# A decoder trunk in split fp32: the order of the long and short products in the FFN's first projection

## The chip, the cores and the metric

The kernel runs on one core of a Trainium2 chip. The metric is device time in microseconds (us). The core has five engines with queues of their own: TensorE (PE in the profile; its weight loads are listed apart as PEld), VectorE (DVE), ScalarE (ACT), GpSimd (POOL) and SyncE (SP), which here only issues DMAs. Each engine takes its instructions strictly in the order that was fixed when the program was built.

## The reference

Two layers on a sequence of 256 tokens of width 1024, in float32. Layer 0 is half an FFN, a gated linear recurrence (HGRN2), half an FFN; layer 1 is half an FFN, dilated attention with shared keys and values, half an FFN. The change lies in the four FFNs:

```python
def _rms(x, gain):
    y = xf * lax.rsqrt(jnp.mean(xf * xf, axis=-1, keepdims=True) + EPS)
    return y * gain

def _swiglu(h, w_in, w_out):
    gate, up = jnp.split(h @ w_in, 2, axis=-1)
    return (jax.nn.silu(gate) * up) @ w_out

x = x + 0.5 * _swiglu(_rms(x, norm_gain[layer, 0]), ffn_w_in[layer, 0], ffn_w_out[layer, 0])
```

`w_in` is 1024 x 5632 (2816 gate columns, then 2816 up columns), `w_out` 2816 x 1024.

## The kernel before

**Split operands.** TensorE is fed with a rounded type (float32r), and the precision of float32 is kept by splitting every operand into a high half (rounded) and a low half (what rounding left). Of the four partial products three are made: high by high, low weight by high input, high weight by low input. A weight tile comes by DMA into a `raw` tile (line 242), ScalarE casts it to the high half `wh` (line 245), VectorE subtracts to get the low half `wl` (line 246). There are 4 `raw` buffers and 6 each of `wh` and `wl`; each holds 2 slices of 128 input channels by 512 columns. A buffer is taken again when its last reader is done: `raw` by the subtraction, `wh` and `wl` by the products. The input `xs` stands as `xs.hl`: per slice of 128 channels, 256 tokens of the high half beside 256 tokens of the low half.

**The first projection of an FFN** runs transposed (`linear_T`, line 275): weights are the stationary operand, tokens stream. It goes in 11 blocks (`c` in `ffn_within`, line 622), each of 256 gate and 256 up columns. A block's output is four accumulators of 128 columns, one PSUM bank each, in two pairs of a gate and an up bank (`spans`): pair 0 and pair 1. Each bank gets, for each of the 8 slices of channels, one *long* product (line 322; `wh` against `xs.hl`, 512 columns, which makes high by high in the bank's left half and high by low in its right half) and one *short* product (line 319; `wl` against the high half, 256 columns, added to the left half). That makes 32 longs and 32 shorts per block. The weights of a block come in four *parts* of two slices: parts 0 and 1 are called early, 2 and 3 late.

**Order of the products before.** In the first block of an FFN the order is special (`first_block` in the first FFN, the branch `norm.used == False` in the others, and in the second block of the first FFN). In every other block it is, for pair 0 and then for pair 1: 8 longs of the early parts, 16 shorts, 8 longs of the late parts. A pair's late longs and the early longs that follow them stand in a row, so PE runs 16 longs, 16 shorts, 16 longs, 16 shorts.

**After a pair's last product** `consume` (line 624) empties its banks: per bank a copy of the right half on ScalarE (line 458) and the addition of the left half on VectorE (line 459). These *sums* are `g` and `u`. Later come a multiplication on GpSimd (line 629), a SiLU on ScalarE (634), a product on GpSimd (635), and the split of the result into `hid` (216 and 217). These are put off by counted `tick()`s, which the product loops call; there are eight per block. The pool of accumulators has four banks, so a block's two pairs hold all of them, and the next block takes a bank when it has been emptied.

**What orders the engines' queues.** The instructions of an engine are put in order when the program is built, by a planner that takes what it thinks ready, what was written earlier first. `tc.issue_after(x)` keeps what is written inside it behind `x` on the engine of `x`. In `linear_T` the loads of part `n` stand inside such a block for every instruction in `norm.ahead[n]`, and `Norm.behind` (line 534) fills that list at the end of each block for the next one: the early parts come after the sums of the last pair of the block before the last (`made`), the late parts after the sums of pair 0 of the last block (`sums[0]`). Each list holds copies and additions, so it binds casts on ScalarE as well as subtractions on VectorE.

After the 11 blocks the second projection (`linear`, line 267, with `products`, line 252) uses the same buffers and banks. The recurrence's `linear_T` calls use the same function.

Of the kernel before, what the change touches and what calls it, by code (L numbers as in the profile page):

```python
# [19 lines left out]
P = 128  # L20
S = 256
NT = S // P
D = 1024
KD = D // P
# [3 lines left out]
NK = 2  # L28
# [75 lines left out]
def trunk(ctx, tc, x_in, norm_gain, ffn_w_in, ffn_w_out, a_w_in, a_lb_logits, a_out_gain, a_w_out,  # L104
          kv_norm, w_kv, k_gain, b_w_q, b_q_gain, b_w_o, rel_bias, c_onehot, c_masks, out):
    nc = tc.nc
# [87 lines left out]
    def tick():  # L194
        for job in pending:
            job[0] -= 1
        for job in [j for j in pending if j[0] <= 0]:
            pending.remove(job)
            job[1]()
# [49 lines left out]
    def accumulators():  # L249
        return [psa.tile([P, 512], F32, tag="acc", name=f"acc{t}") for t in range(NT)]  # L250
# [21 lines left out]
            part = load_part([(c0, v[:, k0 : k0 + nk, :]) for c0, v in columns], nk)  # L272
            products(xs, ps, k0, nk, nkt, *part, consume)

    def linear_T(norm, columns, spans, consume):


        xs = norm.sets[0][1]

        def load(k0):  # L280
            return load_part([(c0, v[:, k0 : k0 + NK, :]) for c0, v in columns], NK)

        starts = range(0, KD, NK)
        blocks, last = range(len(spans)), len(starts) - 1
        half = len(starts) // 2
        early, late = range(half), range(half, last + 1)


        parts = []
        for n, k0 in enumerate(starts):  # L290
            with ExitStack() as order:
                for ins in norm.ahead[n]:
                    order.enter_context(tc.issue_after(ins.ins))
                parts.append(load(k0))
        if norm.used:
            rows = []
            for i in blocks:
                rows += [("L", i, n) for n in early] + [("S", i, n) for n in range(last + 1)] + [("L", i, n) for n in late]
        else:

            rows = [(kind, i, n) for kind in "LS" for i in blocks for n in early]
            rows += [(kind, i, n) for i in blocks for kind in "SL" for n in late]
        norm.used = True
        sums = []


        banks = {}
        for kind, i, n in rows:
            if kind == "L" and n == 0:
                banks[i] = accumulators()  # L310
            ps = banks[i]
            wh, wl = parts[n]
            for k in range(NK):
                xs.need(n * NK + k)
            for c, acc in zip(spans[i], ps):
                for k in range(NK):
                    kk, w = n * NK + k, slice(c, c + P)
                    if kind == "S":
                        nc.tensor.matmul(acc[:, 0:S], wl[:, k, w], xs.h[:, kk, :], start=False, stop=False)  # L319
                    else:  # L320
                        hl = xs.hl[:, kk, :, :].rearrange("p a t -> p (a t)")
                        nc.tensor.matmul(acc, wh[:, k, w], hl, start=kk == 0, stop=kk == KD - 1)  # L322
            if kind == "L":
                if n == last:
                    sums.append(consume(i, ps))
                tick()
        norm.behind(sums)

    def first_block(norm, columns, spans, consume):

# [2 lines left out]
        gain, xs = norm.sets[0]  # L333
# [11 lines left out]
        banks = [accumulators(), [bank("first") for c in spans[1]]]  # L345
# [96 lines left out]
        sums = []  # L442
# [8 lines left out]
        half = KD // NK // 2  # L451
        norm.ahead = [ahead] * half + [ahead + [row] + sums[0] + sums[1]] * half
        norm.made = sums[1]

    def total(acc, pool, tag):

# [5 lines left out]
    class Norm:  # L462


        def __init__(self, x, sets, by_token=True, in_order=False, row_lag=ROW_LAG):
            self.x = x
            self.row_lag = row_lag
            self.spreads = by_token
            self.in_order = in_order
            self.used = False  # L470
            self.ahead = [[] for n in range(KD // NK)]
            self.made = []
            self.sets = [(g, Halves(act, KD, tag)) for g, tag in sets]
            self.fed = 0
            self.r = None
            self.by_token = None
            self.waiting = []
# [53 lines left out]
            if self.spreads and not self.in_order:  # L531
                defer(self.row_lag, self.spread)

        def behind(self, sums):


            half = KD // NK // 2
            self.ahead = [self.made] * half + [sums[0]] * half
            self.made = sums[-1]

        def halve(self):
# [76 lines left out]
    def ffn_within(x, pool, pool2, layer, f, norm, following):  # L618
        w_in = ffn_w_in[layer, f].rearrange("(k p) n -> p k n", p=P)
        hidden = Halves(pool, KF, "hid")  # L620

        for c in range(FC):

            def consume(i, ps, c=c):
                g, first = total(ps[0], pool2, "g")
                u, last = total(ps[1], pool2, "u")

                def scaled():
                    nc.gpsimd.tensor_tensor(g, g, norm.by_token, op=ALU.mult)  # L629
                    defer(SILU_LAG, gated)  # L630
                    defer(HIDDEN_LAG, put)

                def gated():
                    nc.scalar.activation(g, g, AF.Silu)  # L634
                    nc.gpsimd.tensor_tensor(u, u, g, op=ALU.mult)  # L635

                def put():
                    k = 2 * c + i
                    hidden.put(slice(k, k + 1), slice(0, S), u.unsqueeze(1))

                norm.with_rows(scaled)
                return first + last

            a, b = c * 256, DFF + c * 256
            spans = [(0, 256), (P, 256 + P)]
            if layer + f + c == 0:
                first_block(norm, w_in.rearrange("p k (s n) -> p k s n", s=2)[:, :, :, :256], spans, consume)
            else:
                linear_T(norm, [(0, w_in[:, :, a : a + 256]), (256, w_in[:, :, b : b + 256])], spans, consume)

        w_out = ffn_w_out[layer, f]

        def consume(n, t, ps):
            add_to_x(x, n, t, ps, following, norm.half[:, t : t + 1])
            if following is None:
                send(t, slice(n * 512, (n + 1) * 512), nc.sync)

        def send(t, cols, beside):
            for r, queue in enumerate((nc.sync, beside)):
                queue.dma_start(rows_of(out, 2 * t + r)[:, cols], x[64 * r : 64 * r + 64, t, cols])  # L660

        if following is not None:
            for n in range(2):
                linear(hidden, KF, [(0, half_of(w_out, n))], lambda t, ps, n=n: consume(n, t, ps))
            return
        linear(hidden, KF, [(0, half_of(w_out, 0))], lambda t, ps: consume(0, t, ps))


        ps = accumulators()
        parts = []  # L670
        tail = KF - 2 * NK
        for k in range(0, KF, NK):
            part = load_part([(0, half_of(w_out, 1)[:, k : k + NK, :])], NK)
            if k < tail:
                products(hidden, ps, k, NK, KF, *part, None)
            else:
                parts.append(part)
        for k in range(tail, KF):
            hidden.need(k)

        def rest(to, t, w, opens):
            tok = slice(t * P, (t + 1) * P)
            for kk in range(tail, KF):
                wh, wl = (v[:, (kk - tail) % NK, w] for v in parts[(kk - tail) // NK])
                nc.tensor.matmul(to, hidden.h[:, kk, tok], wh, start=opens and kk == tail, stop=False)
                nc.tensor.matmul(to, hidden.h[:, kk, tok], wl, start=False, stop=False)
                nc.tensor.matmul(to, hidden.l[:, kk, tok], wh, start=False, stop=kk == KF - 1)

        def add(t, c0, ps):
            xv = x[:, t, c0 : c0 + ps.shape[-1]]  # L690
            nc.vector.scalar_tensor_tensor(xv, ps, norm.half[:, t : t + 1], xv, op0=ALU.mult, op1=ALU.add)

        rest(ps[0], 0, slice(0, 512), False)
        add(0, 512, ps[0])
        send(0, slice(512, 1024), nc.sync)
        rest(ps[1][:, 0:256], 1, slice(0, 256), False)
        end = bank("end")[:, 0:256]
        rest(end, 1, slice(256, 512), True)
        add(1, 512, ps[1][:, 0:256])
        send(1, slice(512, 768), nc.sync)  # L700
        add(1, 768, ps[1][:, 256:512])
        add(1, 768, end)
        send(1, slice(768, 1024), nc.scalar)


    norm = Norm(x, [(gain_of(0, 0), "xT")], in_order=True)
# [34 lines left out]
    with ExitStack() as hgrn:  # L741
# [6 lines left out]
        w_in = a_w_in[0].rearrange("(k p) n -> p k n", p=P)  # L748
        xs = norm2.sets[0][1]
# [317 lines left out]
        norm = Norm(x_second, [(gain_of(0, 2), "xT")])  # L1067
# [9 lines left out]
    norm = Norm(x, [(gain_of(1, 1), "xT")], by_token=False)  # L1077
    ffn(x, 1, 0, norm2, norm)

    with ExitStack() as attn:  # L1080
# [73 lines left out]
        xs = norm.sets[0][1]  # L1154
# [295 lines left out]
```

## Time and profile before

| | us |
|---|---|
| median of 3 runs (least to most) | 1161.67 (1161.43 to 1161.83) |
| the profiled execution | 1161.63 |
| its span, first to last instruction | 1159.9 |
| TensorE busy | 1152.8 |
| VectorE busy | 781.2 |
| ScalarE busy | 706.8 |
| GpSimd busy | 227.7 |

The granted clock of TensorE was 1.0 on the whole. In the lines of the profile, `acc<-xT,wh x16` means 16 instructions in a row that write an accumulator from `xT` (or `xK`: the input) and `wh`; the first two numbers of a timeline row are the start and the time from the first start to the last end in us; a bracket gives idle time of the engine just before, and what ended it. Matmuls overlap at their ends, so a product's duration is longer than the spacing from one start to the next; the spacing is what counts. L322 is line 322 of the listing.

### The profile page before, as it was taken

Reading aid. Unit: us, or ns where it says so; the run is one execution under the profiler, and the core shown is the slowest. Engines: PE = TensorE matmul, PEld = TensorE weight load, DVE = VectorE, ACT = ScalarE, POOL = GpSimd, SP = SyncE. Lnnn points to the kernel's source line nnn. Section 1 sums busy time; section 2 is a strip of 40 time slices with the busy share of each in tenths; the row PEclk is TensorE's granted clock in tenths of the full one; section 3 lists DMA queues with packets and bytes.
Section 4 is the critical chain, followed back from the end, with each engine's and each line's share of the span. In section 5 each row is a group of like instructions: output and inputs, shape, how many; then the busy total and the mean of one; then the engine's idle time right before and its main releaser. Section 6 shows DMA issues by size and latency. Waiting matters only on the chain.

```text
span 1159.9 us, 18928 instructions
## 1 busy us (share of the span) xinstructions
PE 1152.8 (99%) x6781; PEld 973.1 (84%) x6781; DVE 781.2 (67%) x1276; ACT 706.8 (61%) x1263; POOL 227.7 (20%) x243
## 2 busy tenths in 40 slices
PE   9999999999999999999999999999999999999998
PEld 7888888888888888888888887888877778888887
DVE  6766655898577666657667556866866865766752
ACT  6665555876566655556656446557767775665631
POOL 2323201310023331003333002231210100332300
PEclk9999999999999999999999999999999999999999
DMA  8766656644457666556665666565555453766661
GB/s 254 223 183 200 209 186 191 183 160 164 127 167 212 186 198 203 185 158 202 183 196 190 210 184 190 172 195 176 156 165 152 138 153 103 222 183 183 198 221 54
DMA packets 181731, 209.23 MB, mean 180 GB/s; under 512 B 15499, under 2 KB 139987, under 8 KB 181636
## 3 DMA queue, kind: packets, MB, share of 16 engines
q1 hardware_dynamic: 181008, 207.61, 58.1%
q8 instruction: 53, 0.87, 0.3%
q10 hardware_dynamic: 628, 0.40, 0.1%
q14 instruction: 42, 0.34, 0.1%
HBM read 205.82 MB, written 1.10 MB: 178 GB/s over the span
## 4 chain that ended last, share of the span: by engine, by line
PE 94%; DVE 2%; DMA 1%; ACT 1%; issue 0%; POOL 0%; SPq 0%; DVEq 0%; ACTq 0%; POOLq 0%
PE acc L322 28%; PE acc L260 15%; PE acc L319 15%; PE acc L262 14%; PE acc L261 14%; DVE wl L246 1%; PE ob L1406 1%; DMA raw<-in_ffn_w_in_dram 1%; PE tpn L1148 1%; PE tpp L1381 1%; PE tp L493 1%; ACT wh L245 1%; PE ob L1002 0%; PE wps L162 0%; PE sp L1331 0%
## 5 line engine op out<-in xcount | busy, mean ns | idle before, releaser
L246 DVE TENSOR_TENSOR wl<-raw,wh 128x1024 fp32r<-128x1024 f32 x380 | 479.7, 1271 | 225.4 <-ACT wh L245 163.3
L245 ACT CAST wh<-raw 128x1024 fp32r<-128x1024 f32 x380 | 397.0, 1050 | 198.5 <-PE acc L262 161.1
L322 PE MATMUL acc<-xT,wh 128*128 128x512 f32 x1152 | 278.4, 392 | 0.0
L322 PEld LDWEIGHTS acc<-xT,wh 128*128 128x128 f32 x1152 | 211.0, 188 | 40.5
L319 PEld LDWEIGHTS acc<-xT,wl 128*128 128x128 f32 x1152 | 147.8, 191 | 6.7 <-DVE wl L246 1.0
L319 PE MATMUL acc<-xT,wl 128*128 128x256 f32 x1152 | 150.1, 283 | 0.6 <-DVE wl L246 0.5
L260 PE MATMUL acc<-wh,hid 128*128 128x512 f32 x344 | 134.2, 390 | 0.0
L262 PE MATMUL acc<-wh,hid 128*128 128x512 f32 x344 | 134.2, 390 | 0.0
L261 PE MATMUL acc<-wl,hid 128*128 128x512 f32 x344 | 133.8, 389 | 0.0
L629 POOL TENSOR_TENSOR g<-g,row 128x256 f32<-128x256 f32 x88 | 67.0, 762 | 274.8 <-DVE g L459 256.3
L635 POOL TENSOR_TENSOR u<-u,g 128x256 f32<-128x256 f32 x88 | 89.9, 1022 | 47.0 <-ACT g L634 47.0
L574 POOL TENSOR_TENSOR rs<-var,mhalf 128x8 f32<-128x8 f32 (+1 forms) x32 | 48.5, 1516 | 229.2 <-DVE var L572 229.2
L260 PE MATMUL acc<-wh,xK 128*128 128x512 f32 x224 | 92.2, 412 | 0.0
L262 PE MATMUL acc<-wh,xK 128*128 128x512 f32 x224 | 88.1, 393 | 0.0
L261 PE MATMUL acc<-wl,xK 128*128 128x512 f32 x224 | 87.7, 392 | 0.0
L458 ACT COPY g<-acc 128x256 f32<-128x256 f32 x103 | 37.9, 372 | 80.6 <-PE acc L322 79.4
L322 PE MATMUL acc<-xK,wh 128*128 128x512 f32 x352 | 84.9, 392 | 0.0
L260 PE MATMUL acc<-wh,xT 128*128 128x512 f32 x192 | 77.7, 405 | 0.0
L262 PEld LDWEIGHTS acc<-wh,hid 128*128 128x128 f32 x344 | 64.6, 188 | 13.4
L260 PEld LDWEIGHTS acc<-wh,hid 128*128 128x128 f32 x344 | 64.6, 188 | 13.3
L261 PEld LDWEIGHTS acc<-wl,hid 128*128 128x128 f32 x344 | 64.6, 188 | 13.2
L262 PE MATMUL acc<-wh,xT 128*128 128x512 f32 x192 | 75.3, 393 | 0.0
(207 smaller groups left out, 1403.6 us busy)
## 6 DMA issues: line engine op xcount, KB each, us to landing
raw<-in_ffn_w_in_dram SPq DMA_DIRECT2D x344, 256.0 KB, 3.9
raw<-in_ffn_w_out_dram SPq DMA_DIRECT2D x88, 512.0 KB, 4.5
raw<-in_w_kv_dram SPq DMA_DIRECT2D x72, 256.0 KB, 4.2
raw<-in_a_w_in_dram SPq DMA_DIRECT2D x32, 512.0 KB, 4.3
raw<-in_b_w_q_dram SPq DMA_DIRECT2D x24, 512.0 KB, 3.7
raw<-in_w_kv_dram SPq DMA_DIRECT2D x48, 128.0 KB, 2.4
raw<-in_a_w_out_dram SPq DMA_DIRECT2D x8, 512.0 KB, 4.7
raw<-in_b_w_o_dram SPq DMA_DIRECT2D x8, 512.0 KB, 3.6
```

Source lines behind the costliest of these rows:

```text
L245: nc.scalar.copy(wh[:, :nk, :], raw[:, :nk, :])
L246: nc.vector.tensor_tensor(wl[:, :nk, :], raw[:, :nk, :], wh[:, :nk, :].bitcast(F32), op=ALU.subtract)
L260: nc.tensor.matmul(ps[t], xs.h[:, kk, tok], wh[:, at, :], start=kk == 0, stop=False)
L261: nc.tensor.matmul(ps[t], xs.h[:, kk, tok], wl[:, at, :], start=False, stop=False)
L262: nc.tensor.matmul(ps[t], xs.l[:, kk, tok], wh[:, at, :], start=False, stop=kk == nkt - 1)
L319: nc.tensor.matmul(acc[:, 0:S], wl[:, k, w], xs.h[:, kk, :], start=False, stop=False)
L322: nc.tensor.matmul(acc, wh[:, k, w], hl, start=kk == 0, stop=kk == KD - 1)
L458: copied = nc.scalar.copy(y, acc[:, S : 2 * S])
L493: nc.tensor.transpose(tp[:, c * P : (c + 1) * P], self.x[:, t, at : at + P], ident)
L574: nc.gpsimd.tensor_tensor(r[:, :n], v[:, :n], mhalf[:, :n], op=ALU.pow)
L629: nc.gpsimd.tensor_tensor(g, g, norm.by_token, op=ALU.mult)
L635: nc.gpsimd.tensor_tensor(u, u, g, op=ALU.mult)
```

## The change

In the FFNs' first projection, from the third block of each FFN on (`norm.blocks > 1` at entry), the products are issued by a new function: all 32 longs first, bank by bank (8 slices into one bank, then the next bank, through both pairs), then all 32 shorts, bank by bank; each pair's `consume` comes after its own shorts. `norm.blocks` counts the blocks of an FFN. The recurrence's calls keep the old order.

`behind` changes what the late parts of the next block come after, for blocks that are followed by a block of the new kind: no longer all four sums of pair 0, but only the very last sum of the block (`sums[-1][-1:]`), an addition on VectorE. So the late subtractions follow the block's last sum, and the late casts on ScalarE have no such order any more. `tick()` is called after every four longs, eight times per block, and not among the shorts.

```diff
-    def linear_T(norm, columns, spans, consume):
+    def linear_T(norm, columns, spans, consume, in_rows=False):
...
+        if in_rows and norm.blocks > 1:
+            return whole_rows(norm, parts, spans, consume)
...
-        norm.behind(sums)
+        norm.behind(sums, in_rows)
+
+    def whole_rows(norm, parts, spans, consume):
+
+        xs = norm.sets[0][1]
+        banks = []
+        for pair in spans:
+            ps = accumulators()
+            banks.append(ps)
+            for c, acc in zip(pair, ps):
+                for kk in range(KD):
+                    hl = xs.hl[:, kk, :, :].rearrange("p a t -> p (a t)")
+                    nc.tensor.matmul(acc, parts[kk // NK][0][:, kk % NK, c : c + P], hl, start=kk == 0, stop=False)
+                    if kk % 4 == 3:
+                        tick()
+        sums = []
+        for i, (pair, ps) in enumerate(zip(spans, banks)):
+            for c, acc in zip(pair, ps):
+                for kk in range(KD):
+                    nc.tensor.matmul(
+                        acc[:, 0:S], parts[kk // NK][1][:, kk % NK, c : c + P], xs.h[:, kk, :], start=False, stop=kk == KD - 1
+                    )
+            sums.append(consume(i, ps))
+        norm.behind(sums, True)
...
-        def behind(self, sums):
+        def behind(self, sums, in_rows):
...
             half = KD // NK // 2
-            self.ahead = [self.made] * half + [sums[0]] * half
+            self.blocks += 1
+            late = sums[-1][-1:] if in_rows and self.blocks > 1 else sums[0]
+            self.ahead = [self.made] * half + [late] * half
             self.made = sums[-1]
...
-                linear_T(norm, [(0, w_in[:, :, a : a + 256]), (256, w_in[:, :, b : b + 256])], spans, consume)
+                linear_T(norm, [(0, w_in[:, :, a : a + 256]), (256, w_in[:, :, b : b + 256])], spans, consume, True)
```

`first_block` sets `norm.blocks = 1`, and `Norm` starts it at 0.

More of the change, by code (lines that the diff above doesn't have):

```diff
@@ L453, in first_block @@
         norm.made = sums[1]
+        norm.blocks = 1
     def total(acc, pool, tag):
@@ L472, in __init__ @@
             self.made = []
+            self.blocks = 0
             self.sets = [(g, Halves(act, KD, tag)) for g, tag in sets]
```

## The prediction

> **What bounds the kernel now.** I read the page first: busy times, granted clock, the chain that ended last.
>
> ```profile
> span 1159.9 us, 18928 instructions
> PE 1152.8 (99%) x6781; PEld 973.1 (84%) x6781; DVE 781.2 (67%) x1276; ACT 706.8 (61%) x1263; POOL 227.7 (20%) x243
> ...
> PEclk9999999999999999999999999999999999999999
> ...
> PE 94%; DVE 2%; DMA 1%; ACT 1%; issue 0%; POOL 0%; SPq 0%; DVEq 0%; ACTq 0%; POOLq 0%
> PE acc L322 28%; PE acc L260 15%; PE acc L319 15%; PE acc L262 14%; PE acc L261 14%; DVE wl L246 1%; PE ob L1406 1%; DMA raw<-in_ffn_w_in_dram 1%; PE tpn L1148 1%; PE tpp L1381 1%; PE tp L493 1%; ACT wh L245 1%; PE ob L1002 0%; PE wps L162 0%; PE sp L1331 0%
> ```
>
> TensorE makes up 94% of the chain at full clock, and the two lines that the change reorders, the long products (L322) and the short ones (L319), hold 43% of it. A reordering of PE's work can win only what PE loses between its products. So the second view is the timeline of PE in steady blocks of the first FFN, and narrow windows of it; a clipped window shows the first start, and the time to the last end, of the products inside it. The two rows with slashes are the products' durations (least/median/most, ns).
>
> ```profile
> 66.21 2.08 PE L319 MATMUL acc<-xT,wl 128*128 128x256 f32 x16
> 68.12 3.82 PE L322 MATMUL acc<-xT,wh 128*128 128x512 f32 x16
> 71.77 2.08 PE L319 MATMUL acc<-xT,wl 128*128 128x256 f32 x16
> 73.69 3.82 PE L322 MATMUL acc<-xT,wh 128*128 128x512 f32 x16
> ...
> 69.51 2.43 PE L322 MATMUL acc<-xT,wh 128*128 128x512 f32 x10
> 72.13 1.72 PE L319 MATMUL acc<-xT,wl 128*128 128x256 f32 x13
> 73.69 1.32 PE L322 MATMUL acc<-xT,wh 128*128 128x512 f32 x5
> L322 PE MATMUL acc<-xT,wh x1152: 387/389/499, 19.8 to 633.1; 128*128 128x512 f32 x192
> L319 PE MATMUL acc<-xT,wl x1152: 277/283/386, 23.5 to 631.4; 128*128 128x256 f32 x192
> ```
>
> From start to start, a settled long product takes (2.43 - 0.389) / 9 = 0.2268 us, a short one (1.72 - 0.283) / 12 = 0.1198 us. The first five longs after a run of shorts are slower: (1.32 - 0.389) / 4 = 0.2328 us. So a run of 16 longs takes 71.77 - 68.12 = 3.65 us where 16 settled ones would take 3.63, and a run of 16 shorts takes 1.91 to 1.92, which is 16 x 0.1198. Is the excess paid for each switch or for each product? Runs of other lengths tell, in the second block of the first FFN:
>
> ```profile
> 23.49 3.04 PE L319 MATMUL acc<-xT,wl 128*128 128x256 f32 x24
> 26.36 2.00 PE L322 MATMUL acc<-xT,wh 128*128 128x512 f32 x8
> 28.20 1.11 PE L319 MATMUL acc<-xT,wl 128*128 128x256 f32 x8
> ```
>
> Eight longs take 28.20 - 26.36 = 1.84 us against 8 x 0.2268 = 1.81: the same 0.02 to 0.03 us as for sixteen. Twenty-four shorts take 2.87 us, 24 x 0.1198. A switch from shorts to longs costs some 0.022 us, the other way nothing. That is all that PE loses in a steady block; there is no wait in it.
>
> ```profile
> 64.39:75.52 11.13, 11.13 (x65) 9.84 (x64) 7.40 (x11) 6.84 (x13) 3.55 (x4) 1.00 0.64 189
> ```
>
> In this row of the table by stages (stretch, us, then busy PE, PEld, DVE, ACT, POOL, clock, DMA share, GB/s) one block of 11.13 us has PE busy throughout, VectorE for 7.40 and ScalarE for 6.84 us. They have room, but their deadlines move.
>
> **The change, part by part.**
>
> *Order of the products.* Nothing is added or removed: 32 longs and 32 shorts per block, as before, with the same operands; ticks stay at eight per block, so the deferred steps come up in the same blocks. Before, PE switches to longs twice per block (once per pair), afterwards once. Blocks 2 to 10 of each of the four FFNs take the new path: 9 x 4 = 36. Gain: 36 x 0.022 = 0.8 us (0.7 to 0.9 by the two runs above). Eight products in a row now add to one bank, where it was two; the settled pace is the same across a change of bank as within one, so I cost that at nothing.
>
> *Emptying the banks.* Before, pair 0's banks are emptied under pair 1's 32 products. Now the shorts of all four banks come last, and the next block begins on bank 0 at once. The rows: one bank is emptied by ScalarE's copy and VectorE's addition.
>
> ```profile
> 64.20 0.37 ACT L458 COPY g<-acc 128x256 f32<-128x256 f32 x1 [1.20 <-PE acc L322]
> 64.60 0.42 DVE L459 TENSOR_TENSOR g<-acc,g 128x256 f32<-128x256 f32 x1
> ```
>
> From copy to free bank: 64.60 + 0.42 - 64.20 = 0.82 us. Set the start of a new-style block at 0. Its longs end at 32 x 0.2268 + 0.022 = 7.28, its shorts at 7.28 + 32 x 0.1198 = 11.11. Bank 0's last short ends at 7.28 + 7 x 0.12 + 0.283 = 8.40, and the bank is free at about 9.3 if ScalarE and VectorE are: 1.8 us before the next block wants it. Bank 3's last sum is done at about 11.28 + 0.1 + 0.82 = 12.2, 1.1 into the next block, which wants that bank only after 24 longs (5.4 us). The cover is 1.8 us at bank 0 and 4.3 at bank 3; what lies past it would stall PE in every one of 36 blocks.
>
> *The low halves.* In steady blocks the two late casts and subtractions run before the block that uses them:
>
> ```profile
> 71.83 1.03 ACT L245 CAST wh<-raw 128x1024 fp32r<-128x1024 f32 x1
> 72.89 1.22 DVE L246 TENSOR_TENSOR wl<-raw,wh 128x1024 fp32r<-128x1024 f32 x1 [1.90 <-PE acc L319]
> 73.09 1.05 ACT L245 CAST wh<-raw 128x1024 fp32r<-128x1024 f32 x1
> 74.37 1.22 DVE L246 TENSOR_TENSOR wl<-raw,wh 128x1024 fp32r<-128x1024 f32 x1
> ```
>
> The block that needs them starts at 75.52. Now these subtractions wait for the last sum and run from 1.1 to 3.6 us into their block; its shorts begin at 7.28, so 3.7 us of cover remain. The bracket in the row at 72.89 shows why they must be moved: they reuse buffers that the shorts release, and the shorts now end the block. Queued behind them on VectorE are the next block's two early subtractions and two `hid` ones; four subtractions from 1.1 on end at 1.1 + 4 x 1.22 = 6.0, which leaves 2.9 us for the small ones until bank 0's sum at 8.9. Behind them on SyncE are the reloads of their `raw` buffers, some 3.6 us later in the block than now. The late casts lose their order behind pair 0's copies and are bound only by their buffers, which the last bank's longs release at about 6.1 and 6.5; the first longs that use them come at 0.9 and 1.4 of the next block, where the old order gave until 3.7. In steady blocks 73.09 + 1.05 = 74.14 is early enough. I cost all this at nothing.
>
> *The third block of the second FFN* is not steady:
>
> ```profile
> 346.29 3.82 PE L322 MATMUL acc<-xT,wh 128*128 128x512 f32 x16
> 349.95 2.46 PE L319 MATMUL acc<-xT,wl 128*128 128x256 f32 x16
> ...
> 351.66 0.74 PE L319 MATMUL acc<-xT,wl 128*128 128x256 f32 x4
> ...
> 352.24 0.40 PE L322 MATMUL acc<-xT,wh 128*128 128x512 f32 x1
> 349.11 1.05 ACT L245 CAST wh<-raw 128x1024 fp32r<-128x1024 f32 x1
> 350.39 1.22 DVE L246 TENSOR_TENSOR wl<-raw,wh 128x1024 fp32r<-128x1024 f32 x1
> ```
>
> Its shorts wait for the last part's subtraction (done at 351.61, they go on at 351.66): 352.24 - 349.95 = 2.29 us instead of 1.92, a loss of 0.4 that vanishes, since the shorts now come 5.5 us later. But its longs, which start at 346.29 + 1.84 = 348.13, want that last part's cast after six products, at 349.5, and the cast ends at 350.16: a new wait of 0.7 us, unless it is moved forward. Between 0 and 0.7 I take 0.7, where the row puts it. At the other third blocks the same casts end in time, and the waits in second blocks stay.
>
> **Sum**, on the profiled execution's 1161.63 us (its span of 1159.9 and 1.7 around it; 0.04 below the median of the runs): 1161.63 - 0.8 - 0.4 + 0.7 = 1161.1 us. What a measurement of this kernel can tell from no change is about 0.2%, 2.3 us, so this is no change.
>
> **Rivals.** *The switch is worth nothing.* If the slow first longs belong not to the switch but to what runs beside them, or if the planner mixes shorts among the longs, the 0.8 falls away: 1161.63 - 0.4 + 0.7 = 1161.9 us. Against it: the excess is alike behind 8, 16 and 24 shorts. [...]
>
> *Bank 0 is not free: slower.* The place is ScalarE's queue late in a block. A late cast can stand there ahead of bank 0's copy and wait for its `raw` tile. The rows are the issue of a load on SyncE's queue (ns), and how long loads take from issue to landing, first in steady blocks, then over the whole kernel (least/median/most):
>
> ```profile
> L242 SPq DMA_DIRECT2D raw<-in_ffn_w_in_dram x344: 367/370/1497, 8.5 to 1074.3; - x172
> ...
> DMA to landing us min/median/max: 2.9/3.8/5.0
> DMA to landing us min/median/max: 2.2/3.9/6.0
> ```
>
> The second late subtraction ends at 3.6; its buffer's two loads are issued at about 3.7 and, 0.37 later, 4.1; with 3.8 us the tile lands at 7.9, the cast ends at 8.95, and bank 0 is free at 9.8, in time. With 5.0 it is 11.0, just in time. It decides from a landing of 5.1 us on; at 5.6 each block loses 0.46 us, 36 x 0.46 = 17 us: 1178. For it: four reloads now follow each other closely, at 1.2 us apart, while before they came in pairs. Against it: the medians, and that the copy may stand ahead of the cast. The Trainium skill ("Trainium Kernel Development and Optimization", Best Practices) warns that consistent bubbles can mean that SBUF or PSUM ran out; all four banks are taken by one block here, and no run so far shows a bubble from it.
>
> *Much faster* would need more than PE loses. The waits left in second blocks are these:
>
> ```profile
> 340.15 0.74 PE L319 MATMUL acc<-xT,wl 128*128 128x256 f32 x4 [0.50 <-DVE wl L246]
> 987.86 0.74 PE L319 MATMUL acc<-xK,wl 128*128 128x256 f32 x4 [0.83 <-DVE wl L246]
> ```
>
> The change does not touch these blocks (0.5 + 0.8 us), and what it does touch is 0.8 + 0.4 = 1.2 us. Only a shift in other stages, through another plan, could give more than 0.2%.
>
> **How the numbers follow.** Forecast 0.62; switch worth nothing 0.18; bank 0 late 0.16; a windfall elsewhere 0.04. The first two are within 0.2%, the third above, the fourth below, so faster 0.04, same 0.80, slower 0.16. The forecast's own range is 1160.1 (the cast moves forward, and the switch is worth 0.9, with 0.2 for other stages) to 1162. For 8 in 10 the range takes in the second case and the mild end of the third (0.1 us per block, 3.6 us): 1159.9 to 1165.
>
> **What would show it.** In the changed profile: runs of 32 L322 and 32 L319 in the timeline of PE, a block of 11.11 us, the first five longs of a run slow only once per block. The third block of the second FFN: full pace in its shorts, a wait for the last cast (L245) after six longs. VectorE's late L246 pair straight behind the last L459 of a block. Wrong would be an idle PE ahead of the first long of each block, released by `g` L459 (bank 0), or by `wh` L245, or shorts that wait for L246.

## The result and the profile after

The changed kernel takes 1243.15 us (median, 1241.42 to 1248.07); the kernel before takes 1161.55 (1160.92 to 1161.83) beside it. The ratio is 1.0709, 95% interval 1.0696 to 1.0722: 81.6 us slower, where 1161.1 and no change had been forecast. The profiled execution took 1244.82 us, which is 83.2 more than the profiled one of before.

The same lines of the page as for the kernel before (span, busy times, the chain by engine):

```profile
span 1243.1 us, 19031 instructions
PE 1175.7 (95%) x6781; PEld 983.3 (79%) x6781; DVE 785.1 (63%) x1276; ACT 702.9 (57%) x1263; POOL 238.4 (19%) x243
...
PE 51%; DMA 16%; DVE 11%; ACT 8%; POOL 7%; issue 6%; SPq 1%; ACTq 0%; POOLq 0%; DVEq 0%
```

PE, at 94% of the chain before, holds 51% now. What came in is DMA, VectorE, ScalarE and GpSimd together: a chain that passes through all of them. The view of waits names its joints (who waited for whom: us in total, times, longest):

```profile
PE acc L341 <- DVE g L485: 45.9, 25, 3.6
PE acc L260 <- DVE g L485: 8.9, 4, 2.7
PE acc L260 <- DVE u L485: 3.2, 4, 1.1
...
ACT wh L245 <- DMA raw<-in_ffn_w_in_dram: 120.0, 68, 3.5
```

The first long of a block (L341 in the changed listing) waits for the sum of bank 0 (L485, `g`): the sign that the prediction had named as the one that would prove it wrong. ScalarE's casts wait 120.0 us for tiles of `w_in`; before it was 9.0 us in 11 waits (`ACT wh L245 <- DMA raw<-in_ffn_w_in_dram` there too). The stretches between the first longs of two neighbouring blocks (columns as in the prediction's row) show that PE is idle for 1.82 us of 13.22 in the first, and that none of the other engines is busy for much more than half of it (PEld is PE's own weight loads):

```profile
70.05:83.27 13.22, 11.40 (x65) 9.90 (x65) 7.52 (x11) 6.72 (x12) 3.81 (x4) 1.00 0.56 169
83.27:96.66 13.39, 13.02 (x64) 11.03 (x65) 7.51 (x11) 6.70 (x12) 3.79 (x4) 0.87 0.52 155
```

From the first long of an FFN's third block (its first L341) to the first product of its second projection (L260), the four FFNs take 119.5, 122.4, 116.7 and 117.5 us: 476.1 for 36 blocks, 13.22 each. Before, the same four stretches took 401.2. That is 75.0 of the 83.2 us. It holds the 8.9 us in the second row of the waits, which end at those first products; the 3.2 of the third row come on top. Of the remaining 5.0 some 3 lie in the second projection of the last FFN, where the granted clock stood at 0.50 for 6.83 us (more on that at the end); the rest is spread over the stages around.

Where the loop runs is seen in the timeline of one block, from one copy of bank 0 to the next:

```profile
68.22 1.04 ACT L245 CAST wh<-raw 128x1024 fp32r<-128x1024 f32 x1 [1.74 <-DMA raw<-in_ffn_w_in_dram]
69.17 0.36 ACT L484 COPY g<-acc 128x256 f32<-128x256 f32 x1
...
70.05 7.57 PE L341 MATMUL acc<-xT,wh 128*128 128x512 f32 x32 [1.71 <-DVE g L485]
...
70.91 0.42 ACT L664 ACTIVATE g<-g 128x256 f32<-128x256 f32 x1 [1.10 <-POOL g L659]
71.23 0.36 ACT L484 COPY g<-acc 128x256 f32<-128x256 f32 x1
...
72.18 0.41 ACT L216 CAST hid<-u 128x256 fp32r<-128x256 f32 x1 [0.59 <-POOL u L665]
...
72.49 0.36 ACT L484 COPY u<-acc 128x256 f32<-128x256 f32 x1
...
73.14 0.41 DVE L485 TENSOR_TENSOR u<-acc,u 128x256 f32<-128x256 f32 x1
...
73.47 2.88 DVE L246 TENSOR_TENSOR wl<-raw,wh 128x1024 fp32r<-128x1024 f32 x2
...
76.42 0.37 SPq L242 DMA_DIRECT2D raw<-in_ffn_w_in_dram  x1
...
76.83 0.47 SPq L242 DMA_DIRECT2D raw<-in_ffn_w_in_dram  x1
...
81.44 1.04 ACT L245 CAST wh<-raw 128x1024 fp32r<-128x1024 f32 x1 [2.00 <-DMA raw<-in_ffn_w_in_dram]
82.39 0.36 ACT L484 COPY g<-acc 128x256 f32<-128x256 f32 x1
```

Read it as a round. The copy of bank 0 goes at 69.17. ScalarE takes the copies of pair 1 only behind pair 0's SiLU (L664) and split (L216), each of which waits for GpSimd, so bank 3's copy goes at 72.49: 3.32 us. The last sum (L485, `u`) comes behind it, and the two late subtractions run from 73.47 to 76.35: 3.86 us more. The second one frees a `raw` tile; its two loads are issued at 76.42 and 76.83: 0.48. The cast that waits for that tile goes at 81.44, 4.61 later, and the next copy of bank 0, which stands behind this cast on ScalarE, at 82.39, 0.95 later. 3.32 + 3.86 + 0.48 + 4.61 + 0.95 = 13.22 us: the block. TensorE needs 11.11 us for its products and waits for the rest. No single engine is slow; a chain of small steps returns to its own beginning, and going round it takes longer than the block. There are 28 such rounds, from the third to the tenth block of the four FFNs. Four of the five terms are the same in nearly all of them, to within 0.05 us. The fifth, from the second issue to the cast, goes from 4.07 to 6.42 us (4.61 in the mean), and it makes one round 12.7 us long and another 15.0.

### The profile page after: what moved, and what is told of

Read it like the earlier page. It is cut to its first block, busy times and chain, and to the rows that moved or that the text cites. A ratio compares the mean times of both kernels' runs of the same rounds, so it can differ in the third digit from the quotient of the medians.

```text
span 1243.1 us, 19031 instructions
## 1 busy us (share of the span) xinstructions
PE 1175.7 (95%) x6781; PEld 983.3 (79%) x6781; DVE 785.1 (63%) x1276; ACT 702.9 (57%) x1263; POOL 238.4 (19%) x243
## 4 chain that ended last, share of the span: by engine, by line
PE 51%; DMA 16%; DVE 11%; ACT 8%; POOL 7%; issue 6%; SPq 1%; ACTq 0%; POOLq 0%; DVEq 0%
PE acc L260 13%; PE acc L262 13%; PE acc L261 13%; DMA raw<-in_ffn_w_in_dram 12%; POOL u L665 5%; DVE wl L246 5%; PE acc L324 4%; ACT wh L245 3%; DMA raw<-in_ffn_w_out_dram 3%; PE acc L321 2%; POOL g L659 2%; DVE g L485 1%; DVE u L485 1%; SPq L242 1%; ACT g L484 1%
## 5 line engine op out<-in xcount | busy, mean ns | idle before, releaser
L245 ACT CAST wh<-raw 128x1024 fp32r<-128x1024 f32 x380 | 397.3, 1050 | 338.3 <-PE acc L262 132.8
L341 PE MATMUL acc<-xT,wh 128*128 128x512 f32 x864 | 212.5, 405 | 36.7 <-DVE g L485 35.3
L341 PEld LDWEIGHTS acc<-xT,wh 128*128 128x128 f32 x864 | 165.8, 194 | 77.2 <-DVE g L485 39.4
L485 DVE TENSOR_TENSOR g<-acc,g 128x256 f32<-128x256 f32 x103 | 43.1, 422 | 186.3 <-ACT g L484 186.3
L260 PE MATMUL acc<-wh,hid 128*128 128x512 f32 x344 | 136.3, 396 | 12.1 <-DVE g L485 8.9
L262 PE MATMUL acc<-wh,hid 128*128 128x512 f32 x344 | 135.2, 393 | 0.0
L665 POOL TENSOR_TENSOR u<-u,g 128x256 f32<-128x256 f32 x88 | 101.1, 1150 | 61.2 <-DVE u L485 28.0
L348 PEld LDWEIGHTS acc<-xT,wl 128*128 128x128 f32 x864 | 107.2, 192 | 2.1
L348 PE MATMUL acc<-xT,wl 128*128 128x256 f32 x864 | 107.8, 283 | 0.0
L260 PE MATMUL acc<-wh,xK 128*128 128x512 f32 x224 | 92.3, 412 | 0.0
L260 PEld LDWEIGHTS acc<-wh,hid 128*128 128x128 f32 x344 | 65.1, 189 | 28.2 <-DVE g L485 9.7
L341 PE MATMUL acc<-xK,wh 128*128 128x512 f32 x288 | 69.8, 400 | 11.0 <-DVE g L485 10.6
L260 PE MATMUL acc<-wh,xT 128*128 128x512 f32 x192 | 77.8, 405 | 0.0
```

What stands on the lines that cost most here:

```text
L245: nc.scalar.copy(wh[:, :nk, :], raw[:, :nk, :])
L260: nc.tensor.matmul(ps[t], xs.h[:, kk, tok], wh[:, at, :], start=kk == 0, stop=False)
L262: nc.tensor.matmul(ps[t], xs.l[:, kk, tok], wh[:, at, :], start=False, stop=kk == nkt - 1)
L341: nc.tensor.matmul(acc, parts[kk // NK][0][:, kk % NK, c : c + P], hl, start=kk == 0, stop=False)
L348: nc.tensor.matmul(acc[:, 0:S], parts[kk // NK][1][:, kk % NK, c : c + P], xs.h[:, kk, :], start=False, stop=kk == KD - 1)
L485: return y, [copied, nc.vector.tensor_tensor(y, acc[:, 0:S], y, op=ALU.add)]
```

## The experiments

Theory A is that loop. It has four links: the late casts stand ahead of the copies; the late subtractions follow the last sum; late and early parts share four `raw` tiles; SiLU and split stand between the copies. Cutting or shortening any link should bring the block back to 11.11 us, and lengthening one should lengthen the block by as much. Theory B: four banks are too few where 32 shorts end a block, whatever the other engines do. Theory C: the reloads of `raw` are too crowded, since all four come after the last sum. The first four kernels ran beside each other, and so did the last three; the kernel before took 1161.75 us beside the first and 1161.58 beside the others.

**Late low halves after the first sums.** The new order of the products, with the old rule for the late parts.

```diff
-            late = sums[-1][-1:] if in_rows and self.blocks > 1 else sums[0]
+            late = sums[0]
```

> The new order of products, but the late parts' casts and subtractions come after the four sums of pair 0 again, as before. Theory A (the loop: on ScalarE the late casts now stand ahead of bank 0's copy and wait for raw tiles that come free only after the block's last sum, so that the time around, 13.2 us, takes the place of the block's 11.1): the copies of banks 0 and 1 come first again, a block takes 11.1 us, 1160 to 1164 us in all. Theory B (four banks: closing all four at the end of a block leaves too little time to empty them, whatever ScalarE's order): no better than 1230. Theory C (the four reloads in a row crowd each other and land late): one subtraction moves ahead, so perhaps half is won, about 1200.

Measured: 1166.07 us, ratio 1.0035 (1.0022 to 1.0048). The second link and the first are cut: the late casts are back behind pair 0's copies. A steady block, and the copy and sum of its bank 0:

```profile
63.73:74.85 11.12, 11.12 (x67) 9.85 (x66) 8.42 (x11) 6.53 (x13) 4.85 (x4) 1.00 0.65 191
```

```profile
63.73 7.44 PE L341 MATMUL acc<-xT,wh 128*128 128x512 f32 x32
...
72.22 0.37 ACT L484 COPY g<-acc 128x256 f32<-128x256 f32 x1 [2.60 <-PE acc L348]
72.63 0.42 DVE L485 TENSOR_TENSOR g<-acc,g 128x256 f32<-128x256 f32 x1 [1.70 <-ACT g L484]
```

PE is busy throughout, and all steady blocks last 11.11 us. In a steady block the order of the products alone costs nothing and needs no more than four banks: B falls. The copy now waits for PE, not for ScalarE's own queue. The 4.3 us that this kernel loses lie elsewhere. Three of the last blocks are longer (12.02, 12.01 and 11.45 us), which holds the first of the two waits below, at the start of the second projection; the second wait comes on top, and the third block of the second FFN takes 11.97 us, where it took 11.47 before:

```profile
PE acc L260 <- DVE g L485: 1.7, 3, 0.7
PE acc L260 <- DVE u L485: 1.5, 3, 1.1
```

**Late casts behind the copies, late subtractions still behind the last sum.** One link cut and no other: the list binds a cast by the copies in it, a subtraction by the sums.

```diff
-            late = sums[-1][-1:] if in_rows and self.blocks > 1 else sums[0]
+            late = sums[0] + sums[-1][-1:] if in_rows and self.blocks > 1 else sums[0]
```

> The change whole, with one order put back: the late casts stay behind the copies of pair 0, the late subtractions behind the last sum. Theory A: PE does not wait for bank 0, blocks of 11.1 us, 1160 to 1164 us. Theory B: no better than 1230. Theory C: the reloads still come in a row after the last sum, so the longs wait for the late casts instead, still above 1200.

Measured: 1168.31 us, ratio 1.0056 (1.0040 to 1.0073). All but one of the steady blocks last 11.11 us (that one 11.14), although the late subtractions run where they ran in the changed kernel, behind the last sum (65.43 to 68.33 in a block that starts at 63.97), and all four reloads behind them; the loads of `w_in` take 4.0 us from issue to landing (median) here and in the changed kernel. C falls as the cause. The position of two casts on ScalarE is worth the whole 2.1 us per block. What this kernel loses sits in the main at the four steps from the last block to the second projection, where PE waits for `u` L485 for 1.84, 1.28, 1.76 and 1.71 us; the first of them:

```profile
132.21 1.04 ACT L245 CAST wh<-raw 128x1024 fp32r<-128x1024 f32 x1 [2.21 <-DMA raw<-in_ffn_w_out_dram]
133.16 0.36 ACT L484 COPY u<-acc 128x256 f32<-128x256 f32 x1
...
134.03 0.50 PE L260 MATMUL acc<-wh,hid 128*128 128x512 f32 x1 [1.84 <-DVE u L485]
```

The same mechanism once more, with other tiles: a cast of `w_out` stands ahead of the last block's copy and waits for its load, and PE waits for the bank. The kernel before empties half of the banks under the last products of the block, and it has no wait at this place.

**`raw` tiles of their own for the late parts.** The changed kernel whole, with four more `raw` tiles in the FFNs; the order on ScalarE and VectorE stays.

```diff
...
-        raw = wraw.tile([P, NK, 512], F32, tag="raw", name="raw")
+        pool = late_raw[-1] if late else wraw
+        raw = pool.tile([P, NK, 512], F32, tag="raw", name="raw")
...
+            late_raw.append(pool3)
...
```

(`late` is true for parts 2 and 3 in the FFNs; `pool3` holds four tiles.)

> The change whole, with the same order on ScalarE and VectorE, but the late parts load into four raw tiles of their own, so that their loads need not wait for the subtractions of the block before. Theory A: the loop is cut at the raw tiles, the late casts run without a wait although they still stand ahead of bank 0's copy; 1160 to 1166 us. Theory B: unchanged, 1235 to 1250. Theory C: the loads are started a block ahead, so late landing is hidden too; it can't be told from A here.

Measured: 1162.87 us, ratio 1.0010 (1.0001 to 1.0020), and 11.11 us for every steady block. A late cast still stands ahead of bank 0's copy, but its tile is there long before:

```profile
61.63 0.37 ACT L487 COPY g<-acc 128x256 f32<-128x256 f32 x1 [0.37 <-PE acc L351]
...
65.93 2.89 DVE L249 TENSOR_TENSOR wl<-raw,wh 128x1024 fp32r<-128x1024 f32 x2
...
70.38 2.00 ACT L248 CAST wh<-raw 128x1024 fp32r<-128x1024 f32 x2 [1.25 <-PE acc L344]
...
72.74 0.37 ACT L487 COPY g<-acc 128x256 f32<-128x256 f32 x1 [0.37 <-PE acc L351]
```

From bank 0's copy to the end of the late subtractions it takes 65.93 + 2.89 - 61.63 = 7.19 us here and 73.47 + 2.88 - 69.17 = 7.18 in the changed kernel. So this part of the round was no consequence of the delay; it is what the queues take in any case. What differs is only whether somebody ahead of the next copy waits for it. The blocks win 1.2 us in all (401.2 to 400.0). The kernel is still 1.1 us slower than the one before, with one new wait of 1.3 us in a second projection (for `u` L488 again) and smaller losses that were not taken apart.

**The four copies together.** The changed kernel, with SiLU placed behind the block's last copy, which shortens the way from bank 0's copy to bank 3's.

```diff
+        latest = []
...
+                latest[:] = last[:1]
...
                 def gated():
-                    nc.scalar.activation(g, g, AF.Silu)
+                    with tc.issue_after(latest[0].ins):
+                        nc.scalar.activation(g, g, AF.Silu)
```

(`latest` holds the copy of the pair's second bank. The SiLUs are put off, so by then it is the copy of the fourth bank.)

> The change whole, but the SiLUs come after the block's last copy on ScalarE, so that the copies of pair 1 no longer stand behind a SiLU and a split that wait for GpSimd. The late casts still stand ahead of bank 0's copy. Theory A: the last sum comes 2.0 to 2.8 us sooner after bank 0's copy, so the time around falls from 13.2 to 10.4 to 11.2 us, below or about the block's own 11.1: 1160 to 1170 us. Theory B: the copies still start as late, 1230 or more. Theory C: reloads as crowded as before and landing as late, above 1220.

Measured: 1185.17 us, ratio 1.0210 (1.0192 to 1.0227): the total was missed, the blocks were not.

```profile
63.75 0.36 ACT L484 COPY g<-acc 128x256 f32<-128x256 f32 x1
...
65.17 0.37 ACT L484 COPY u<-acc 128x256 f32<-128x256 f32 x1 [0.51 <-PE acc L348]
...
73.79 1.05 ACT L245 CAST wh<-raw 128x1024 fp32r<-128x1024 f32 x1 [1.65 <-DMA raw<-in_ffn_w_in_dram]
74.74 0.36 ACT L484 COPY g<-acc 128x256 f32<-128x256 f32 x1
```

Bank 3's copy follows bank 0's after 1.42 us instead of 3.32, and the round takes 74.74 - 63.75 = 10.99 us, just under a block. The cast still waits for its tile ahead of the copy, and it costs nothing, or next to it: the fourth to tenth blocks of the FFNs last 11.11 to 11.22 us but for one of 11.49. Most of the loss is in the last block of each FFN (13.86, 14.05, 14.60 and 14.93 us, which holds 7.5 us of waits of `PE acc L260` for `g`), and in the 4.6 us for which L260 waits for `u` behind it. Why the transitions are so much worse here than in the kernels above was not taken apart.

**One addition in the loop.** The changed kernel whole, and one more VectorE addition of 128x512, on data that nobody reads, between the last sum and the late subtractions.

```diff
...
+                junk = tmp4.tile([P, 512], F32, tag="s5", name="junk")
+                with tc.issue_after(sums[-1][-1].ins):
+                    xs = self.x[:, 0, 0:512]
+                    late = [nc.vector.tensor_tensor(junk, xs, xs, op=ALU.add)]
```

> The change whole, with one VectorE addition of 128x512 on data that nobody reads put between the last sum of a block and the late low halves of the next (from the third block on). It adds work and leaves nothing out. Theory A: the addition lies in the loop, so each block lasts longer by what it takes, about 0.4 to 0.65 us; 36 blocks give 14 to 23 us, 1257 to 1268 in all, with the longs of each block waiting longer by the same. If the block's length is set by anything that does not pass through the late subtractions (the four banks, the reloads' own pace, ScalarE's queue alone), VectorE has 5.7 us idle in each 13.2 us block and the addition is hidden: 1242 to 1246.

Measured: 1265.09 us (1264.33 to 1269.01), 21.9 more than the changed kernel. The addition's row (duration: least/median/most, ns), the wait of the first longs, and a stretch between two blocks:

```profile
L572 DVE TENSOR_TENSOR junk<-res x30: 674/677/1187, 382.2 to 1203.9; 128x512 f32<-128x512 f32 x30
```

```profile
PE acc L341 <- DVE g L485: 66.3, 30, 4.7
```

```profile
75.27:89.10 13.83, 13.83 (x65) 11.71 (x65) 8.12 (x12) 6.70 (x12) 3.24 (x4) 0.81 0.49 150
```

VectorE is busy for 8.12 of 13.83 us, so there was room to hide 0.68 us anywhere but in the loop. It was not hidden. In the 28 rounds from bank 0's copy to the next one (third to tenth block), the stretch from the last sum's start to the end of the late subtractions takes 3.82 us in the mean where it took 3.22: 0.60 more for 0.677 added. The rounds themselves take 14.24 us where they took 13.24, because the step from the second issue to the cast is longer too, 5.00 us for 4.61; why the loads take longer here is open. The 36 blocks, counted as above, take 499.9 us, 13.89 each against 13.22. That this 0.66 is so near to the addition is in part chance, since the last blocks are shorter here (11.47, 12.74, 12.08 and 12.85 us; 14.31, 13.07, 14.65 and 14.44 in the changed kernel). The longs wait 66.3 - 45.9 = 20.4 us more. (In this stretch PE is busy throughout, at a mean clock of 0.81; more on that at the end.)

**The old order, with the late rule alone.** Does a late subtraction behind the last sum cost as much in the order of before?

```diff
-            late = sums[0]
+            late = sums[-1][-1:] if self.blocks > 1 else sums[0]
```

> This kernel keeps the order of the products of the kernel before, four runs of longs and shorts in a block, and takes over from the change only the rule that the late low halves of a block follow the last sum of the block before, here from the second block of each FFN on. Theory A (the loop: the bank 0 copy waits behind a late cast, the cast for a raw tile that only the late subtraction frees, and that subtraction for a sum that the copy feeds): in this order the late casts stand behind the copies of pair 0, so the loop is not closed by them; what is left is that the products of the late parts need low halves that start about 1 us into the block, where the first short of part 2 comes about 2.8 us into it. I expect some tenths to 1 us of waiting in each of 36 blocks, 1170 to 1200 us in all, and the waits in front of a short rather than in front of a long. A rival, that any late low half behind the last sum costs 2 us a block whatever the order of the products: about 1235 to 1245. If the low halves land in time in this order, 1161 to 1163.

Measured: 1209.44 us, ratio 1.0418 (1.0402 to 1.0434): 47.9 us, 1.33 per block in the mean, above what the theory had given and far below its rival. Two third blocks, of the first and the second FFN, hold 9 us of it (16.16 and 15.81 us long); the usual block is 1.2 us longer. The kind of wait is as expected:

```profile
72.92 3.34 DVE L246 TENSOR_TENSOR wl<-raw,wh 128x1024 fp32r<-128x1024 f32 x2
...
73.78 1.58 PE L319 MATMUL acc<-xT,wl 128*128 128x256 f32 x12
...
76.31 0.73 PE L319 MATMUL acc<-xT,wl 128*128 128x256 f32 x4 [0.95 <-DVE wl L246]
```

There is no loop, but a plain lateness: twelve shorts run, and the last four wait until the subtractions end at 76.26; the gap is 0.95 us, and a block lasts 12.34 us there (70.13 to 82.47) for 11.13. The two subtractions take 3.34 us here where the prediction's rows have 1.22 each. With those they would have ended at 75.36, about when the twelve shorts ran out, which is why the estimate was low. So the late rule needs the new order, in which shorts start 7.28 us into the block; and in the new order its harm comes by another way.

**Whole rows in the fourth to the tenth block only.** The new order with the old rule for the late parts; the third and the eleventh block in the old order.

```diff
-        if in_rows and norm.blocks > 1:
+        if in_rows:
...
-            late = sums[-1][-1:] if in_rows and self.blocks > 1 else sums[0]
+            late = sums[0]
...
-                linear_T(norm, [(0, w_in[:, :, a : a + 256]), (256, w_in[:, :, b : b + 256])], spans, consume, True)
+                linear_T(norm, [(0, w_in[:, :, a : a + 256]), (256, w_in[:, :, b : b + 256])], spans, consume, 3 <= c < FC - 1)
```

> The order of the change (32 longs, 32 shorts) in the fourth to the tenth block of each FFN alone, the low halves following the first sums as in the kernel before; the third and the last block keep the old order. If the steady block is worth 11.11 for 11.13 us and the losses of the run with early low halves all lie at the third block of the second FFN and at the step from the last block to the second projection, then 28 blocks at 0.022 us give 0.6 us and nothing is lost: 1161.0, between 1160.7 and 1161.5, beside 1161.6 for the kernel before. If the transitions still lose 0.3 to 1.2 us each because the tenth block itself runs in the new order: 1162 to 1165.

Measured: 1161.22 us (1160.45 to 1161.94) beside 1161.58 (1160.74 to 1162.51) for the kernel before; ratio 0.9997 (0.9988 to 1.0006), which cannot be told from no change. The trace has the small gain where it was expected:

```profile
53.22 7.44 PE L341 MATMUL acc<-xT,wh 128*128 128x512 f32 x32
60.50 4.00 PE L348 MATMUL acc<-xT,wl 128*128 128x256 f32 x32
64.33 7.44 PE L341 MATMUL acc<-xT,wh 128*128 128x512 f32 x32
```

64.33 - 53.22 = 11.11 us, no bracket on any row, and so in each of the 24 stretches between two new blocks; the transitions lose nothing. This is all that the order of the products has to give: 28 x 0.02 = 0.6 us by the stretches, 0.36 by the medians.

## Why the prediction was wrong, point by point

*Order of the products*: right, in size too. Wherever nothing else holds PE, a block lasts 11.11 us for 11.13, one switch saved; eight products in a row on one bank cost nothing, as assumed. The rival that the switch is worth nothing is refuted by the same rows.

*Emptying the banks*: right for bank 0 as far as PE goes, wrong for bank 3. "Free at about 9.3 if ScalarE and VectorE are" is what the run with the early low halves shows: the sum ends at 72.63 + 0.42, 9.32 us after the block's start. The condition in that half sentence is what failed in the changed kernel, where the copy stood behind a cast that was waiting. The last sum was put 1.1 us into the next block, from the last short's end alone. In the changed kernel it ends at 73.14 + 0.41 = 73.55, 3.5 us into the block, because the copies of pair 1 stand behind SiLU and split, which wait for GpSimd. The prediction had taken the copies to follow each other.

*The low halves*: this is the step that failed. "Now these subtractions wait for the last sum and run from 1.1 to 3.6 us into their block", with the reloads behind them and the casts "bound only by their buffers", all costed "at nothing". They ran from 3.4 to 6.3 us. The cover was measured against the shorts that need the low halves, and that cover held: no short of the new order waits in a steady block. It was not measured against what else hangs on the subtractions, the `raw` tile that they free, whose next cast had just been let go from its place behind the copies. The late casts were said to lose their order as if that were a freedom; on an engine that takes its instructions in order it meant a place ahead of the copies.

*Rival "Bank 0 is not free"*: the mechanism was the right one, with the right place, and its price was a fifth of the true one (17 us, from 0.46 per block, against 82). It had made a landing of 5.1 us the point that decides. Loads had become only a little slower: the median from issue to landing was 4.0 us for 3.9 before, and from the second issue to the cast it took 4.61 us in the block shown and in the mean, 0.8 more than the prediction's sum has and inside its spread. What was late was the issue, 76.83 instead of 70.05 + 4.1 = 74.15. And the rival was worked as one pass with some cover, not as a round. With the way over ScalarE's queue in it (3.32 us from bank 0's copy to bank 3's), the prediction's own remaining durations give about 3.3 + 0.8 + 2.5 + 0.5 + 3.8 + 1.05 = 11.95 us, already more than 11.11 (the rest up to 13.22 is the load, 0.8, and the sum and the subtractions, 0.6); once a round is longer than the block, each block lasts as long as the round, and no cover is left to count on. "Against it: ... that the copy may stand ahead of the cast" was an open question that the trace of before couldn't answer, and it should have weighed more than 0.16. The Trainium skill's sentence that was set beside the rival ("Trainium Kernel Development and Optimization", Best Practices), that consistent bubbles can mean that SBUF or PSUM ran out, is borne out here in part: PE waits ahead of 25 of the 32 blocks from the fourth on, 1.8 us in the mean, and four more `raw` tiles in SBUF remove it. So does the order of two casts with the same tiles, and it was not PSUM's four banks.

*Third block of the second FFN*: right. Its longs stop after six, for the last cast:

```profile
368.34 1.54 PE L341 MATMUL acc<-xT,wh 128*128 128x512 f32 x6
370.41 3.92 PE L341 MATMUL acc<-xT,wh 128*128 128x512 f32 x16 [0.53 <-ACT wh L245]
```

370.41 - (368.34 + 6 x 0.2268) = 0.71 us for the 0.7 forecast.

*What the prediction did not name*: the step from the last block to the second projection. Its waits were 12.1 us in the changed kernel (8.9 + 3.2), and it was the largest loss left in three of the experiments (late low halves after the first sums, late casts behind the copies, the four copies together). A block that empties all of its banks at its end also hands them over late to the work that follows it.

## What to carry to other kernels

When a wait is moved, follow not only who reads its result but which buffers it frees, who reloads them, and where the first reader of the reload stands in its engine's queue; if that path returns to the start, add it up as a round and compare it with the time of one pass, since a round that is longer sets the pace by itself. Removing an order from an engine with one queue does not remove waiting: the instruction gets a place, and everything behind it waits with it. A test that costs little is a small dose of work in the suspected loop, on an engine with time to spare: if the rounds get longer by it, it lies on the path that sets the pace. Compare it step by step, since a total can agree by chance.

## What the runs showed of the hardware beside this

The granted clock fell behind short waits of PE. In the changed kernel, the longs of the block at 70.05, behind a wait of 1.71 us, took 7.40 us up to the first short; those at 83.27, behind 1.82 us, took 9.02, at a mean clock of 0.87 in that stretch:

```profile
83.27 9.19 PE L341 MATMUL acc<-xT,wh 128*128 128x512 f32 x32 [1.82 <-DVE g L485]
92.29 3.99 PE L348 MATMUL acc<-xT,wl 128*128 128x256 f32 x32
```

Six of 32 blocks are like it (8.98 to 9.05 us), in the kernel with the addition in the loop thirteen (8.83 to 10.25), in the kernels whose blocks have no waits none. The Trainium skill ("TensorE: Matmul & The Clock Gate", "What's actually happening") has the clock fall after at least one idle window of about 3.4 us, counted by a clock of its own; here idle stretches of about half of that were enough at times, and the block at 396.21, behind a wait of 3.24 us, still has its longs in 7.39. And these slow longs cost nothing visible: the block at 83.27 lasted 13.39 us, the block at 110.21, with longs of 8.99, 12.85, no longer than the others. While a loop outside PE sets the pace, a lower clock only fills the wait with slower work. It is part of why PE's busy time rose by 22.9 us with the same instructions. Where PE sets the pace, the lower clock does cost: in the last FFN's second projection, behind the wait of 2.39 us for `g`, the clock stood at 0.50 from 1176.26 to 1183.09, and its products took 58.7 us from the first start to the last end, where they took 54.6 before; 1.1 of the difference is the wait for `u`.
